# Stick-breaking values for 512 queries at a time, from turned weights in a triangular layout, with moved loads

## The chip, the core and the metric

The kernel runs on one core of one Trainium2 chip. The metric is the device time of one execution in microseconds. Of the kernel before, three runs were timed, and one more execution was profiled.

## The reference

One decoder layer, for 1024 positions of width 1024, in float32. An input projection feeds a gated linear attention (GLA, 4 heads) and a stick-breaking attention (8 heads of width 128); both are gated, projected, merged by learned gates, projected again, added to the input and normalized. Cut to what the change touches:

```python
# stick_breaking: q, k, v of 8 heads, d = 128, for blocks of 128 queries
z = einsum('bhqd,bhkd->bhqk', qb, kh[:, :, :L]) / sqrt(d)
causal = spos < tpos
log1m = where(causal, log_sigmoid(-z), 0.0)
between = cumsum(log1m, axis=3, reverse=True) - log1m
A = where(causal, exp(log_sigmoid(z) + between), 0.0)
o = einsum('bhqk,bhkd->bhqd', A, vh[:, :, :L])
...
o_sb = o_sb * silu(s_gate)                 # gate: another projection of h
merged = gates[0] * (o_gla @ w_pa) + gates[1] * (o_sb @ w_pb)
x = rmsnorm(x + merged @ w_o, final_g)
```

So a query's weight of a key is sigmoid(z) times the product of sigmoid(-z) over the keys between the two.

## The kernel before, in words

Float32 accuracy is reached with pairs: every operand is split into a rounded part (`h`) and what is left (`l`), by a copy on ACT (line 161) and a subtraction on DVE (line 162), and a product is three matmuls, h·h, h·l and l·h. The normalized input, turned, lies in four quarters `ha11`, `ha12`, `ha21`, `ha22`, each 128 x 4 x 512 for h and l.

The stages follow each other. First come the norm, the value projections and the sums S1 to S4 of the quarters. Then, to about 719 us, `Pairs`: 28 jobs of two 128-column groups by a seven-product scheme (units `u` = 0 to 6; unit 2 is the one that reads S2, line 284), with the GLA work laid between them. S1 to S4 lie in the pool `sp`; the quarter `ha21` is not read by the pairs, lies in DRAM meanwhile (`d_a21`), and comes back by two transfers of 1 MB (line 897) into a pool that is opened after `sp` is closed.

Then the stick-breaking stage, 64 steps of (head h, block i of 128 queries). A step has three parts on PE. `scores(h, i)` makes z against the keys before it, in one piece up to 512 keys and two above; ACT makes sigmoid(-z) in `eb` (line 935) and sigmoid(z) in `be` (936), DVE scans `eb` backwards into the running product (939), POOL masks the diagonal block of `be` (940), DVE multiplies (943). `turn(h, i)` turns `be` by blocks of 128 (line 958) and splits them into `ath`, `atl`. `values(h, m)` multiplies them with v for 256 queries (975 to 977), takes the gate times the result (978) and stores it. Scores run two steps ahead of the turn. Between them stand units of projection (24 matmuls of 512 columns, lines 200 to 202), taken from one long list: gates of the stick-breaking heads, then the GLA projection `w_pa`. How many stand where is written in `SB_PLAN`: for each i, so many ahead of the turn, and so many behind it. A unit's weights are loaded by `load_w` (line 177) into one of two `raw` tiles.

Last come `w_pb` with the merge, and the output projection by the seven-product scheme, with the residual x in tiles `y`, `ya` (`y_load`, line 1218), the add (1243), the sum of squares, the scale and the stores.

Within these stages a tile scheduler sets the order in which each engine gets its instructions, starting from the order of the program; in a few stretches (`manual_schedule`) ACT and DVE, in the last one PE too, keep the order written. Each engine then works through its own list in order, and each DMA is issued in the order of SP's list. A tile that takes another's place waits until the other is read.

Of the kernel before, what the change touches and what calls it, by code (L numbers as in the profile page):

```python
# [15 lines left out]
P = 128  # L16
# [19 lines left out]
SB_PLAN = [(0, 0), (0, 0), (0, 0), (0, 1), (0, 0), (0, 0), (1, 0), (0, 1)]  # L36
# [63 lines left out]
def hybrid_layer(ctx: ExitStack, tc: tile.TileContext, x, norm_g, w_in, w_up, b_dec,  # L100
# [73 lines left out]
    def load_w(w, c0, eng=nc.vector):  # L174

        raw = raw_tile()[:, :, 0:P]
# [147 lines left out]
    SLOTS = ["s2h", "s2l", "s1h", "s1l", "s3h", "s3l", "s4h", "s4l"]  # L324

    def slot(i, shape, name, dt=F32):

        n = math.prod(shape[1:])
        return (sp.tile([P, 4, HALF], dt, tag=SLOTS[i], name=name, bufs=1)
                .rearrange("p a b -> p (a b)")[0:shape[0], 0:n])  # L330
# [565 lines left out]
    for i in range(2):  # L896
        nc.sync.dma_start(hq[1, 0][i].bitcast(F32), d_a21[i])
    sb = sr_ctx.enter_context(tc.tile_pool(name="sb", bufs=2, side="right", reuse_waits="tile"))
# [46 lines left out]
    def turn(h, i):  # L945

        be = bets.pop((h, i))
        ath, atl = abuf[(i // 2 + 1) % 2]
        qc = slice((i % 2) * P, (i % 2 + 1) * P)
        s0 = 1 - i % 2  # L950
        nb = i + 1
        for b0 in range(0, nb, 4):
            bn = min(4, nb - b0)
            pt = (ps.tile([P, HALF], F32, tag="pp", name="pp", bufs=3) if b0 else
                  ps.tile([P, HALF], F32, tag="tr", name="tr"))
            for b in range(bn):
                c = T - (b0 + b + 1) * P
                nc.tensor.transpose(pt[:, b * P:(b + 1) * P], be[:, c:c + P], ident)  # L958
            ss = slice(s0 + b0, s0 + b0 + bn)
            split(pt[:, 0:bn * P].rearrange("p (a b) -> p a b", a=bn),  # L960
                  ath[:, ss, qc], atl[:, ss, qc])

    def values(h, m):

        ath, atl = abuf[(m + 1) % 2]
        v = vts[h]
        gs = slice(m * DV, (m + 1) * DV)
        gate = ev.tile([P, HALF], F32, tag="f", name="f")[:, 0:DV]
        nc.sync.dma_start(gate, d_sg[h][:, gs])
        pav = ps.tile([P, HALF], F32, tag="av", name="av", bufs=1)  # L970
        ns = 2 * m + 2
        for s in range(ns):
            j = 2 * m + 1 - s
            vh, vl = (v[j // 4][:, j % 4, e] for e in range(2))
            nc.tensor.matmul(pav[:, 0:DV], vh, ath[:, s], start=s == 0, stop=False)  # L975
            nc.tensor.matmul(pav[:, 0:DV], vh, atl[:, s], start=False, stop=False)  # L976
            nc.tensor.matmul(pav[:, 0:DV], vl, ath[:, s], start=False, stop=s == ns - 1)  # L977
        nc.vector.tensor_mul(gate, pav[:, 0:DV], gate)
        nc.sync.dma_start(d_osb[h][:, gs], gate)
# [18 lines left out]

    def load(w, c0, key):
# [377 lines left out]
```

## Time and profile before

| | |
|---|---|
| median of 3 runs | 1217.54 us (1216.15 to 1218.54) |
| profiled execution, its own time | 1220.86 us |
| its span, first to last instruction | 1219.1 us |
| PE (matmul) busy | 1202.0 us, 99% |
| DVE busy | 793.8 us, 65% |
| ACT busy | 540.7 us, 44% |
| mean DMA rate | 198 GB/s |
| granted TensorE clock, mean | 0.996 |

PE is TensorE's matmuls, PEld its weight loads, DVE VectorE, ACT ScalarE, POOL GpSimd, SP the engine that issues nearly all DMAs. In a group's row stand line, engine, operation, the names out<-in, shapes and count; then busy us and mean ns of one; then the idle time ahead of them and what ended it. In a row of a stretch stand its bounds, its length, the busy time of PE, PEld, DVE, ACT and POOL (with counts), the granted clock, the DMA engines' share and GB/s. A row in order of time has start, length, engine, line and operation; in brackets the idle time before it.

### The profile page before, as it was taken

The numbers are of one execution on the slowest core, as the hardware profiler recorded it, in microseconds if no ns is written. First come the engines' busy times: TensorE is split into PE (matmuls) and PEld (weight loads), VectorE is DVE, ScalarE is ACT, GpSimd is POOL, SyncE is SP. The second block draws the span as 40 slices with busy tenths as digits, with TensorE's granted clock in tenths as the row PEclk, the third lists the DMA queues.
The fourth block names the chain that finished last, engine by engine and source line by source line (L and its number), as shares of the span: only waits on it lengthen the run. The fifth ranks groups of instructions, "written<-read, shape, count | busy, mean of one in ns | idle before, by whom it ended". The sixth has DMA issues, their size and how long they took to land.

```text
span 1219.1 us, 17810 instructions
## 1 busy us (share of the span) xinstructions
PE 1202.0 (99%) x6327; PEld 1019.6 (84%) x6327; DVE 793.8 (65%) x1285; ACT 540.7 (44%) x1045; POOL 323.3 (27%) x303
## 2 busy tenths in 40 slices
PE   8999999999999999999999999999999999999997
PEld 8999878888888888888888878888888888888876
DVE  5575875675766566766765437777687875345676
ACT  5344663334334444454443325454455554332343
POOL 1495523322422324223223211111121110033201
PEclk9999999999999999999999999999999999999999
DMA  7544348866656547657554395545896636667653
GB/s 278 186 143 140 147 169 293 278 205 190 203 155 203 175 143 231 201 191 228 171 180 146 118 321 165 191 141 163 277 300 218 198 131 226 199 213 248 243 192 121
DMA packets 209236, 241.41 MB, mean 198 GB/s; under 512 B 12758, under 2 KB 152044, under 8 KB 207100
## 3 DMA queue, kind: packets, MB, share of 16 engines
q1 hardware_dynamic: 208572, 239.23, 60.0%
q8 instruction: 50, 0.82, 0.3%
q10 hardware_dynamic: 576, 1.05, 0.2%
q14 instruction: 38, 0.31, 0.1%
HBM read 149.53 MB, written 90.70 MB: 197 GB/s over the span
## 4 chain that ended last, share of the span: by engine, by line
PE 83%; issue 7%; DVE 4%; ACT 2%; DMA 2%; POOL 1%; SPq 0%; POOLq 0%; ACTq 0%; DVEq 0%
PE pp L266 13%; PE pp L268 13%; PE pp L267 13%; PE pp L219 8%; PE pp L202 6%; PE pp L201 5%; PE pp L200 5%; PE tr L958 1%; PE xb L1235 1%; PE xb L1236 1%; PE xb L1234 1%; PE av L976 1%; POOL be L940 1%; PE pp L1234 1%; DVE eb L939 1%
## 5 line engine op out<-in xcount | busy, mean ns | idle before, releaser
L940 POOL TENSOR_SCALAR_AFFINE_SELECT be<-be 128x128 f32<-128x128 f32 x64 | 44.9, 701 | 235.4 <-ACT be L936 204.3
L305 DVE TENSOR_TENSOR f<-pp,f 128x512 f32<-128x512 f32 x84 | 57.9, 689 | 73.3 <-PE pp L268 67.8
L162 DVE TENSOR_TENSOR wl<-tt,wh 128x1024 fp32r<-128x1024 f32 x56 | 69.6, 1243 | 53.1 <-ACT wh L161 52.8
L162 DVE TENSOR_TENSOR wl<-raw,wh 128x1024 fp32r<-128x1024 f32 x55 | 75.9, 1381 | 42.6 <-ACT wh L161 41.8
L161 ACT ACTIVATE wh<-raw 128x1024 fp32r<-128x1024 f32 x55 | 58.1, 1058 | 93.7 <-PE pp L267 47.0
L939 DVE TENSOR_TENSOR_SCAN eb<-eb,m 128x128 f32<-128x128 f32 (+3 forms) x64 | 86.8, 1358 | 15.8 <-ACT eb L935 15.7
L240 POOL TENSOR_TENSOR tt<-raw 128x512 f32<-128x512 f32 x28 | 39.1, 1397 | 205.1 <-DVE wl L162 198.5
L161 ACT ACTIVATE wh<-tt 128x1024 fp32r<-128x1024 f32 x56 | 59.3, 1059 | 67.9 <-PE pp L267 67.3
L272 ACT ACTIVATE f<-pp 128x512 f32<-128x512 f32 x84 | 49.7, 592 | 79.5 <-PE pp L268 76.2
L227 POOL TENSOR_TENSOR r<-r,nhalf 128x1 f32<-128x1 f32 x40 | 24.3, 607 | 191.9 <-DVE r L226 178.5
L935 ACT ACTIVATE eb<-z 128x384 f32<-128x384 f32 (+4 forms) x96 | 48.0, 500 | 47.0 <-issue 22.0
L585 ACT ACTIVATE o<-o,vcol 128x512 f32<-128x512 f32 x32 | 23.0, 724 | 62.0 <-DMA o<-d_gb 40.4
L943 DVE TENSOR_TENSOR be<-be,eb 128x128 f32<-128x128 f32 (+3 forms) x64 | 48.3, 756 | 3.1 <-DVE eb L939 0.5
L200 PE MATMUL pp<-bh,wh 128*128 128x512 f32 x128 | 49.8, 389 | 0.0
L201 PE MATMUL pp<-bl,wh 128*128 128x512 f32 x128 | 49.8, 389 | 0.0
L202 PE MATMUL pp<-bh,wl 128*128 128x512 f32 x128 | 49.8, 389 | 0.0
L936 ACT ACTIVATE be<-z 128x384 f32<-128x384 f32 (+4 forms) x96 | 48.3, 503 | 0.0
L976 PE MATMUL av<-atl,v 128*128 128x256 f32 x160 | 46.0, 288 | 2.0 <-DVE atl L162 2.0
L975 PE MATMUL av<-ath,v 128*128 128x256 f32 x160 | 47.3, 295 | 0.0
L1125 POOL TENSOR_TENSOR f<-m 128x512 f32<-128x512 f32 x8 | 14.2, 1771 | 118.8 <-DVE m L1115 118.8
L977 PE MATMUL av<-ath,v 128*128 128x256 f32 x160 | 45.3, 283 | 0.0
L266 PE MATMUL pp<-ha22h,wh 128*128 128x512 f32 x112 | 44.5, 397 | 0.2 <-DVE f L305 0.2
(430 smaller groups left out, 4014.9 us busy)
## 6 DMA issues: line engine op xcount, KB each, us to landing
raw<-in_w_in_dram SPq DMA_DIRECT2D x31, 1024.0 KB, 6.2
d_v<-o SPq DMA_DIRECT2D x32, 256.0 KB, 2.9
d_gv<-o SPq DMA_DIRECT2D x32, 256.0 KB, 3.6
v<-d_gv SPq DMA_DIRECT2D x32, 256.0 KB, 3.0
d_ogl<-o SPq DMA_DIRECT2D x64, 128.0 KB, 2.5
d_q<-o SPq DMA_DIRECT2D x16, 512.0 KB, 4.8
d_k<-o SPq DMA_DIRECT2D x16, 512.0 KB, 4.1
k<-d_k SPq DMA_DIRECT2D x8, 1024.0 KB, 5.6
```

Source lines behind the costliest of these rows:

```text
L161: nc.scalar.activation(hi, src, AF.Copy)
L162: eng.tensor_sub(lo, src, hi.bitcast(F32))
L200: nc.tensor.matmul(pt, whi[:, kb], h_, start=kb == 0, stop=False)
L201: nc.tensor.matmul(pt, whi[:, kb], l_, start=False, stop=False)
L202: nc.tensor.matmul(pt, wlo[:, kb], h_, start=False, stop=kb == KB - 1)
L219: nc.tensor.matmul(pt[:, 0:n], *ops[kb][i], start=k == 0, stop=k == 3 * KB - 1)
L266: nc.tensor.matmul(pt, bh[:, j], ah[:, j], start=first and j == 0, stop=False, skip_group_check=True)
L267: nc.tensor.matmul(pt, bh[:, j], al[:, j], start=False, stop=False, skip_group_check=True)
L268: nc.tensor.matmul(pt, bl[:, j], ah[:, j], start=False, stop=j == 3, skip_group_check=True)
L305: nc.vector.tensor_add(add, bank, add)
L939: nc.vector.tensor_tensor_scan(rest, rest, m1[:, off:T][:, ::-1], 1.0, op0=ALU.mult, op1=ALU.max)
L976: nc.tensor.matmul(pav[:, 0:DV], vh, atl[:, s], start=False, stop=False)
```

## The change

**Values by 512 queries.** `values(h, g)` takes a group g of four blocks. For the second group, the four key blocks of the first group are products of 512 columns (`far`). In the group's own four blocks, key block k has queries only from block k on: 512, 384 and 256 columns, and 256 again for the last, of which the first 128 are zeros. The weights lie in `near` as 13 blocks of 128, row k behind row k-1 in steps of three, so that block (k, q) stands at 3k + q and each row is one contiguous run; block 11 is set to zero once. `turn` writes the own group's blocks from a `tr` bank and the far ones from a `pp` bank. There are two `near` pairs, one for each group; that of the first lies in the tiles `tt` and `raw` that the pairs have left. The two weight loads in flight take the two halves of the other `raw` tile. Queries are loaded for two blocks at once, into the tiles `dh` and `dl` of the pairs. `SB_PLAN` is another: three units a head as before, now one each behind the turns of blocks 2, 4 and 7.

**The fourth quarter.** S2 lies in a pool `a21b` that stays open, and `ha21` takes its place: its load is given out four units before the end of the pairs, ahead of the first head's k and v.

**The last residual rows.** The rows of (1, 3) get the tiles `dh` and `dl`, and are loaded with the others; residual rows are loaded, scaled and stored by halves of 512 columns.

In the lists of the engines this is what stands at three places. First PE, at the end of a head of the stick-breaking stage; `z` are scores, `tr` and `pp` from `ident,be` turns, `pp` from `ha..,wh` a unit. Before, from the last score matmul of block 7 on:

```order
L933 MATMUL z<-k,q 128x512
L958 MATMUL tr<-ident,be 128x128 x4
L958 MATMUL pp<-ident,be 128x128 x2
L931 MATMUL z<-k,q 128x256
L932 MATMUL z<-k,q 128x256
L933 MATMUL z<-k,q 128x256
L200 MATMUL pp<-ha11h,wh 128x512
L201 MATMUL pp<-ha11l,wh 128x512
L202 MATMUL pp<-ha11h,wl 128x512
```

The rest of that unit follows, 24 matmuls in all, then the turn of block 6, 18 value matmuls, one score of the next head, and the turn of block 7. Now, from the same matmul on:

```order
L946 MATMUL z<-k,q 128x512
L968 MATMUL tr<-ident,be 128x128 x2
L968 MATMUL pp<-ident,be 128x128 x4
L944 MATMUL z<-k,q 128x256
L945 MATMUL z<-k,q 128x256
L946 MATMUL z<-k,q 128x256
L968 MATMUL tr<-ident,be 128x128 x3
L968 MATMUL pp<-ident,be 128x128 x4
L944 MATMUL z<-k,q 128x256
L945 MATMUL z<-k,q 128x256
L946 MATMUL z<-k,q 128x256
L968 MATMUL tr<-ident,be 128x128 x4
```

The turn of block 7 (last row) has moved to directly behind the turns of 5 and 6 and two scores; the unit stands behind it. In some heads a third score stands before the last row.

DVE at the same place, from the gate product of the values on. Before, and then now:

```order
L978 TENSOR_TENSOR f<-av,f 128x256
L939 SCALAR_TENSOR_TENSOR eb_7321<-eb_7321,m_7322 128x1024
L162 TENSOR_TENSOR atl_7333<-tr,ath_7332 128x4x128
L943 TENSOR_TENSOR be<-be,eb_7321 128x1024
L162 TENSOR_TENSOR atl_7333<-pp,ath_7332 128x2x128
```

```order
L162 TENSOR_TENSOR wl<-raw,wh 128x1024
L566 TENSOR_TENSOR o<-pp,o 128x512
L992 TENSOR_TENSOR f<-av,f 128x512
L952 SCALAR_TENSOR_TENSOR eb_7319<-eb_7319,m_7320 128x1024
L162 TENSOR_TENSOR atl<-tr,ath 128x2x128
L956 TENSOR_TENSOR be<-be,eb_7319 128x1024
```

Between scan and product of block 7 one low part of the turned weights stands in both; it has 256 columns now, 512 before.

SP, at the load of the fourth quarter, before and then now:

```order
L897 DMA ha21h<-d_a_166 128x2048
L578 DMA d_ga_149<-f 128x512
L578 DMA d_ga_148<-f 128x512
L897 DMA ha21l<-d_a_167 128x2048
L177 DMA raw<-in_w_in_dram 128x8x128
L565 DMA d_sg_100<-o 128x512
L886 DMA q<-d_q_76 128x2x128 x3
```

```order
L899 DMA ha21h<-d_a_166 128x2048
L899 DMA ha21l<-d_a_167 128x2048
L580 DMA d_ga_149<-f 128x512 x2
L891 DMA q<-d_q_76 128x2x256
L580 DMA d_ga_148<-f 128x512
L891 DMA q<-d_q_76 128x2x256
```

Both parts of the quarter now stand ahead of the last stores of the pairs, the first queries behind them.

The diff, cut to its core:

```diff
-SB_PLAN = [(0, 0), (0, 0), (0, 0), (0, 1), (0, 0), (0, 0), (1, 0), (0, 1)]
+SB_PLAN = [(0, 0), (0, 0), (0, 1), (0, 0), (0, 1), (0, 0), (0, 0), (0, 1)]
...
+    a21b = ctx.enter_context(tc.tile_pool(name="a21b", bufs=1, side="right", reuse_waits="tile"))
     s_ctx = ExitStack()
...
-                comb[nm] = quarter(sp, nm, nm.lower())
+                comb[nm] = quarter(a21b, nm, "a21") if nm == "S2" else quarter(sp, nm, nm.lower())
...
-    def load_q(h, i):
-        qts[h, i] = sl.tile([P, 2, P], F32R, tag="q", name="q", bufs=3)
-        nc.sync.dma_start(qts[h, i].bitcast(F32), d_q[h][:, :, i * P:(i + 1) * P])
+    def load_q(h, m):
+
+        tag = "d" + "hl"[m % 2]
+        t = sw.tile([P, 4, P], F32R, tag=tag, name="q", bufs=1).rearrange("p a c -> p (a c)")
+        t = t.rearrange("p (s c) -> p s c", s=2)
+        nc.sync.dma_start(t.bitcast(F32), d_q[h][:, :, m * DV:(m + 1) * DV])
+        for e in range(2):
+            qts[h, 2 * m + e] = t[:, :, e * P:(e + 1) * P]
...
-    load_head(0)
-    for s in range(3):
-        load_q(*steps[s])
-    pairs.run()
-    s_ctx.close()
-    a21b = ctx.enter_context(tc.tile_pool(name="a21b", bufs=1, side="right", reuse_waits="tile"))
+    pairs.run(7 * len(pairs.jobs) - 4 - pairs.at)
     hq[1, 0] = quarter(a21b, "ha21", "a21")
     for i in range(2):
         nc.sync.dma_start(hq[1, 0][i].bitcast(F32), d_a21[i])
+    load_head(0)
+    pairs.run()
+    for m in range(2):
+        load_q(0, m)
+    s_ctx.close()
...
-    abuf = [tuple(sb.tile([P, KB - 2 * i, 2 * P], F32R, tag=f"at{s}{i}", name=f"at{s}{i}", bufs=1)
-                  for s in "hl") for i in range(2)]
-    for pair in abuf:
+    wraw = raw_tile()
+    near = [(sw.tile([P, 4 * HALF], F32R, tag="tt", name="ath", bufs=1),
+             sw.tile([P, 4 * HALF], F32R, tag="raw", name="atl", bufs=2)),
+            tuple(sb.tile([P, 13 * P], F32R, tag="at" + s, name="at" + s, bufs=1) for s in "hl")]
+    near = [[a[:, 0:13 * P].rearrange("p (b c) -> p b c", c=P) for a in pair] for pair in near]
+    far = [sb.tile([P, 4, HALF], F32R, tag="af" + s, name="af" + s, bufs=1) for s in "hl"]
+    for pair in near:
         for a in pair:
-            nc.gpsimd.memset(a[:, 0, 0:P].bitcast(F32), 0.0)
+            nc.gpsimd.memset(a[:, 11].bitcast(F32), 0.0)
...
     def turn(h, i):
 
         be = bets.pop((h, i))
-        ath, atl = abuf[(i // 2 + 1) % 2]
...
+        g, q = divmod(i, 4)
+        L = (i + 1) * P
+
+        def go(tag, keys, dst):
+            pt = ps.tile([P, HALF], F32, tag=tag, name=tag, bufs=BANKS.get(tag, 2))
+            for b, k in enumerate(keys):
+                c = T - L + k * P
                 nc.tensor.transpose(pt[:, b * P:(b + 1) * P], be[:, c:c + P], ident)
...
+            split(pt[:, 0:len(keys) * P].rearrange("p (a b) -> p a b", a=len(keys)), *dst)
+
+        go("tr", range(4 * g, i + 1), [a[:, q:4 * q + 1:3] for a in near[g]])
+        if g:
+            go("pp", range(4), [a[:, :, q * P:(q + 1) * P] for a in far])
+
+    def values(h, g):
+
         v = vts[h]
...
+        ops = [(k, pav, far[0][:, k], far[1][:, k]) for k in range(4)] if g else []
+        for k in range(4):
+            q = min(k, 2)
+            ops.append((4 * g + k, pav[:, q * P:HALF],
+                        *(a[:, 3 * k + q:3 * k + 4].rearrange("p b c -> p (b c)") for a in near[g])))
+        for s, (k, out_, ah, al) in enumerate(ops):
...
+            nc.tensor.matmul(out_, vh, ah, start=first, stop=False, skip_group_check=True)
+            nc.tensor.matmul(out_, vh, al, start=False, stop=False, skip_group_check=True)
+            nc.tensor.matmul(out_, vl, ah, start=False, stop=last, skip_group_check=True)
+        nc.vector.tensor_mul(gate, pav, gate)
+        nc.sync.dma_start(d_osb[h][:, half(g)], gate)
...
-        if s + 3 < len(steps):
-            load_q(*steps[s + 3])
+        if i % 2 and s + 3 < len(steps):
+            h2, i2 = steps[s + 3]
+            load_q(h2, i2 // 2)
...
-        if i % 2 == 0 and s:
-            values(*((h, i // 2 - 1) if i else (h - 1, 3)))
-    values(SB_H - 1, 3)
+        if i % 4 == 0 and s:
+            values(*((h, 0) if i else (h - 1, 1)))
+    values(SB_H - 1, 1)
...
     def y_load(n, t):
-        ys[n, t] = (po.tile([P, D], F32, tag="ya", name="ya", bufs=4) if n == 0 or t == 3 else
-                    py.tile([P, D], F32, tag="y", name="y"))
...
+        if (n, t) == (1, 3):
+            ys[n, t] = [sw.tile([P, 4, P], F32, tag="d" + s, name="yd", bufs=1).rearrange("p a c -> p (a c)")
+                        for s in "hl"]
...
-    for t in range(3):
+    for t in range(4):
         y_load(1, t)
...
-        if k == 15:
-            y_load(1, 3)
```

Lines behind the change move: 200 to 202 stay, the scores' 931 to 933 are 944 to 946, the scan 952, the product 956, the transposes 968, the values 989 to 991.

More of the change, by code (lines that the diff above doesn't have):

```diff
@@ L947, in turn @@
         be = bets.pop((h, i))
-        ath, atl = abuf[(i // 2 + 1) % 2]
[L949 to L961, printed above, removed]
@@ L966, in values @@
+        if g:
+            go("pp", range(4), [a[:, :, q * P:(q + 1) * P] for a in far])
+    def values(h, g):
         v = vts[h]
-        gs = slice(m * DV, (m + 1) * DV)
-        gate = ev.tile([P, HALF], F32, tag="f", name="f")[:, 0:DV]
-        nc.sync.dma_start(gate, d_sg[h][:, gs])
+        gate = ev.tile([P, HALF], F32, tag="f", name="f")
+        nc.sync.dma_start(gate, d_sg[h][:, half(g)])
         pav = ps.tile([P, HALF], F32, tag="av", name="av", bufs=1)
[L971 to L977, printed above, removed]
@@ L978, in values @@
-        nc.vector.tensor_mul(gate, pav[:, 0:DV], gate)
-        nc.sync.dma_start(d_osb[h][:, gs], gate)
+        ops = [(k, pav, far[0][:, k], far[1][:, k]) for k in range(4)] if g else []
[4 more added lines that the diff above has]
+        for s, (k, out_, ah, al) in enumerate(ops):
+            vh, vl = (v[k // 4][:, k % 4, e] for e in range(2))
+            first, last = s == 0, s == len(ops) - 1
+            nc.tensor.matmul(out_, vh, ah, start=first, stop=False, skip_group_check=True)
+            nc.tensor.matmul(out_, vh, al, start=False, stop=False, skip_group_check=True)
+            nc.tensor.matmul(out_, vl, ah, start=False, stop=last, skip_group_check=True)
@@ L997, in hybrid_layer, with go @@
     ws = {}
+    wk = []
     def load(w, c0, key):
-        return (lambda: ws.__setitem__(key, load_w(w, c0)), False)
+        def go():
+            raw = wk.pop(0) if wk else None
+            ws[key] = load_w(w, c0, raw=raw)
+            if raw is not None:
+                wk.append(raw)
+        return (go, False)
     def unit(key, quads, n, fn):
@@ L1046, in hybrid_layer @@
     st = Line(line)
+    wk += [wraw.rearrange("p k c -> p (k c)")[:, i * KB * P:(i + 1) * KB * P].rearrange("p (k c) -> p k c", c=P)
+           for i in range(2)]
     st.run(2)
@@ L1214, in y_load @@
     def y_load(n, t):
[L1215 to L1216 removed]
+        if (n, t) == (1, 3):
+            ys[n, t] = [sw.tile([P, 4, P], F32, tag="d" + s, name="yd", bufs=1).rearrange("p a c -> p (a c)")
+                        for s in "hl"]
+        else:
+            y = (po if n == 0 else py).tile([P, D], F32, tag="y", name="y", bufs=4 - n)
+            ys[n, t] = [y[:, half(J)] for J in range(2)]
         r0 = n * HALF + t * P
[L1218 removed]
+        for J in range(2):
+            nc.sync.dma_start(ys[n, t][J], x2[r0:r0 + P, half(J)])
     for t in range(4):
```

42 lines of the change are left out of this document (20 added, 22 removed).

## The prediction

> **What bounds the kernel now.** I read the span and the shares of busy time first.
>
> ```profile
> span 1219.1 us, 17810 instructions
> PE 1202.0 (99%) x6327; PEld 1019.6 (84%) x6327; DVE 793.8 (65%) x1285; ACT 540.7 (44%) x1045; POOL 323.3 (27%) x303
> ```
>
> PE is busy for 1202.0 of 1219.1 us, so two things alone move the end: PE time that is saved, and PE time that stands still. DVE, with 65%, has slack on average; whether it has any at one place must be read there. So next came the waits of PE from 690 to 1060 us, the whole stick-breaking stage with what leads into it (waited for, total, times, longest), and then stretches of 5 and 10 us around each wait, with PE's busy time in the second column and the granted clock in the third from the end.
>
> ```profile
> PE av L976 <- DVE atl L162: 2.0, 7, 0.3
> PE pp L201 <- DMA ha21l<-d_a: 2.0, 1, 2.0
> ```
>
> ```profile
> 725.00:730.00 5.00, 3.00 (x16) 2.14 (x16) 3.75 (x7) 2.47 (x7) 1.60 (x3) 1.00 0.91 310
> 730.00:735.00 5.00, 5.00 (x16) 3.95 (x15) 0.00 (x0) 0.00 (x0) 0.00 (x0) 0.66 0.69 217
> 770.00:775.00 5.00, 4.73 (x29) 3.81 (x29) 3.29 (x5) 3.07 (x8) 1.52 (x2) 1.00 0.78 266
> 1180.00:1190.00 10.00, 9.26 (x41) 7.34 (x40) 6.75 (x10) 2.62 (x4) 0.55 (x1) 1.00 0.36 141
> 10.00:20.00 10.00, 7.36 (x39) 6.34 (x38) 7.16 (x11) 5.30 (x10) 1.10 (x2) 0.83 1.05 405
> ```
>
> Little is left to win from waits: 2.0 us for the fourth input quarter, seven of about 0.3 us at the second value matmul, and one of 0.74 us near the end (1180 to 1190). But a wait can cost more than its length. After the 2.0 us wait the stretch from 730 to 735 ran at a mean clock of 0.66; if the low clock is half, that is 0.34/0.5 x 5 = 3.4 us at half rate, or 1.7 us of PE work lost. The matmuls show it: they follow at about 0.23 us before, and at 0.43 us in it.
>
> ```profile
> 729.18 0.50 PE L201 MATMUL pp<-ha21l,wh 128*128 128x512 f32 x1 [1.99 <-DMA ha21l<-d_a]
> ...
> 730.57 0.63 PE L200 MATMUL pp<-ha21h,wh 128*128 128x512 f32 x1
> 731.00 0.63 PE L201 MATMUL pp<-ha21l,wh 128*128 128x512 f32 x1
> ```
>
> The stretch 10 to 20 us, with 2.64 us of PE idle, shows the same sign (0.83: 1.7 us lost). Waits of 0.3 and 0.74 us leave the clock at 1.00. So somewhere between 0.74 and 2.0 us of standing still, about 1.7 us more has to be paid.
>
> **The change part by part. Values by 512 queries.** What a matmul costs is the distance to the next start, since they overlap. The first row below is one of the three groups of value matmuls, the others are starts.
>
> ```profile
> L976 PE MATMUL av<-atl,v 128*128 128x256 f32 x160 | 46.0, 288 | 2.0 <-DVE atl L162 2.0
> ```
>
> ```profile
> 790.22 0.39 PE L200 MATMUL pp<-ha12h,wh 128*128 128x512 f32 x1
> ...
> 792.03 0.39 PE L202 MATMUL pp<-ha12h,wl 128*128 128x512 f32 x1
> 793.14 0.28 PE L976 MATMUL av<-atl,v 128*128 128x256 f32 x1
> ...
> 795.06 0.28 PE L977 MATMUL av<-ath,v 128*128 128x256 f32 x1
> ```
>
> Eight starts of 512 columns take 1.81 us, 0.226 each; sixteen of 256 take 1.92, 0.120 each; 384 columns, halfway between, I take at 0.173. Before: 480 value matmuls of 256 (three lines, 160 each) are 57.6 us. Now each head has 18 of 512, 6 of 384 and 12 of 256: 4.07 + 1.04 + 1.44 = 6.55 us, and eight heads 52.4. PE saves **5.2 us**. The number of transposes, of score matmuls and of projection matmuls is the same. The halved number of gate loads, value stores and gate products takes work from SP, DMA and DVE, which do not bound on average: nothing by itself.
>
> **The seven waits at the second value matmul** go: the diagonal values now start a whole step and 24 projection matmuls after the transposes of their last block, and no longer right behind them. **2.0 us** saved.
>
> **The fourth input quarter** is loaded into the place of the sum S2 as soon as the third product of the last pair has read it, and its second part no longer waits for the sums' pool to be given up.
>
> ```profile
> 708.29 0.39 PE L268 MATMUL pp<-S2h,wl 128*128 128x512 f32 x1
> ...
> 721.31 0.42 SPq L897 DMA_DIRECT2D ha21l<-d_a  x1
> ...
> 724.84 0.39 PE L200 MATMUL pp<-ha21h,wh 128*128 128x512 f32 x1
> ```
>
> ```profile
> ha21l<-d_a SPq DMA_DIRECT2D x1, 1024.0 KB, 7.8
> ```
>
> The last reading of S2 starts at 708.29; a transfer of 7.8 us issued then lands around 716 and the second one, sharing the engines, some microseconds later, before PE wants the quarter at 724.84. Now the second part is issued at 721.31. The wait of 2.0 and the half clock of 1.7 go: **3.7 us**. What hides the load are the last four units of that pair; if SP comes to the issue late, up to the same 3.7 stays.
>
> **The last residual rows** get two tiles of their own and are loaded with the others. At present their transfer starts when an output store has landed, the add that needs it comes late, and PE waits:
>
> ```profile
> 1182.88 0.33 SPq L1218 DMA_DIRECT2D ya<-in_x_dram  x1
> ...
> 1187.19 0.50 PE L1234 MATMUL pp<-wB22h,mS4h 128*128 128x512 f32 x1 [0.74 <-DVE ya L1243]
> ```
>
> **0.7 us** saved. Handling rows by halves adds eight loads, four stores and four products on DVE, with the same bytes and columns, at a place where PE waits for nothing else. I take nothing for it; the final products stand off PE's path behind the last matmul as before.
>
> Saved in all: 5.2 + 2.0 + 3.7 + 0.7 = **11.6 us**.
>
> **The new table of units.** This is what costs. Of a head's eight steps, 0 to 7, the units of projection stand behind the turns of steps 2, 4 and 7 now; the one ahead of step 6's turn is gone. So between the scores of step 7 (1024 keys) and the transposes of its weights, PE has two turns and two small scores, no projection. Before, a whole unit and 18 value matmuls stood there too. The present trace gives the length of both sides:
>
> ```profile
> 855.40 0.39 PE L933 MATMUL z<-k,q 128*128 128x512 f32 x1
> 855.63 0.60 PE L958 MATMUL tr<-ident,be 128*128 128x128 f32 x4
> 856.15 0.61 ACT L935 ACTIVATE eb<-z 128x512 f32<-128x512 f32 x1
> 856.32 0.39 PE L931 MATMUL z<-k,q 128*128 128x256 f32 x1
> 856.54 0.28 PE L932 MATMUL z<-k,q 128*128 128x256 f32 x1
> ...
> 857.40 2.28 DVE L939 TENSOR_TENSOR_SCAN eb<-eb,m 128x1024 f32<-128x1024 f32 x1
> ...
> 860.17 1.22 DVE L943 TENSOR_TENSOR be<-be,eb 128x1024 f32<-128x1024 f32 x1
> 861.31 0.42 DVE L162 TENSOR_TENSOR atl<-pp,ath 128x256 fp32r<-128x256 f32 x1
> 862.27 0.60 PE L958 MATMUL tr<-ident,be 128*128 128x128 f32 x4
> ...
> 862.95 0.36 PE L975 MATMUL av<-ath,v 128*128 128x256 f32 x1
> ...
> 865.55 0.60 PE L958 MATMUL tr<-ident,be 128*128 128x128 f32 x4
> ```
>
> The chain, from the start of the last score matmul (855.40): the second sigmoid ends at 856.76, 1.36 later; the scan takes 2.28, a low part of 256 columns, which now stands between scan and product on DVE, 0.42, the product 1.22: 5.28, less some 0.1 for each of two DVE instructions that start before the one ahead has ended (861.31 begins before 860.17 + 1.22): 5.1 us. In the present order the product ended at 861.39 and the transposes came at 865.55; 4.2 us of slack. PE's cover in the new order: the last score and six transposes, 855.40 to 856.32, 0.92; a 256-wide score, 0.46 (0.22 for its first matmul, 0.12 for two more); seven transposes, 0.68 (862.27 to 862.95); one more 256-wide score, 0.46. Together 2.52 us. **PE stands still for 5.1 - 2.5 = 2.6 us in each head.** In the last head no scores of a next one follow, the cover is 0.92 + 0.68 = 1.6, and it waits 3.5. Seven times 2.6 and 3.5: **21.7 us** lost. Behind the waiting transposes stand, in PE's one queue, the 24 matmuls of the unit, so nothing fills the hole. From below, with the low part of 256 hidden and no delay between engines, the chain is 0.39 + 0.61 + 2.28 + 1.22 = 4.5 and the wait 2.0, 17 us in all; from above, a DVE that has just begun a split of weights (the row below) when the scan is due would make it 3.8, 31 us. I stay at 21.7, since in the printed order that split stands three places ahead of the scan.
>
> ```profile
> L162 DVE TENSOR_TENSOR wl<-tt,wh 128x1024 fp32r<-128x1024 f32 x56 | 69.6, 1243 | 53.1 <-ACT wh L161 52.8
> ```
>
> **The clock.** Each new wait is longer than the 2.0 us that was followed by 3.4 us at half rate. A wait that falls into two of the clock's stretches may escape, so I count six of eight at 1.6 us: **9.6 us**, as an estimate; none and all (13.6) are the ends. Here the Trainium skill says otherwise: by its page "TensorE: Matmul & The Clock Gate", "Why this matters for your kernels", only gaps of more than about 3 us between matmuls drop the rate. Here a wait of 1.99 us was followed by the half rate, so the trace does not agree; by the page's rule seven of the eight waits would cost only their length.
>
> Sum against the profiled execution: -11.6 + 21.7 + 9.6 = +19.7 us. Its span of 1219.1 becomes 1238.8. That execution took 1220.9 us, 3.3 above the median of the runs shown (1217.5), so the median becomes 1237.2, **1237 us**.
>
> **The rivals.** *The waits come, the clock holds.* For it: a wait that is cut by the edge of a clock stretch, and the seven short waits without effect. Against it: both places with about 2 us of idle PE lost clock. It gives -11.6 + 21.7 = +10.1: 1227.6 us. The rule of the Trainium skill's page "TensorE: Matmul & The Clock Gate" leads to this outcome too.
>
> *The cover suffices after all: faster.* The place is the turn of step 7; the mechanism would be a chain that ends within PE's cover. It decides where the wait and its lost clock fall below 11.6/8 = 1.45 us a head, a chain under 4.0 us without any lost clock. For it: DVE is at 65%, and the slack is 4.2 us now. Against it: the four durations alone sum to 4.5, and the scan, one instruction over 1024 columns, can't begin before the last sigmoid. Price: all 11.6 us, 1205.9.
>
> *The quarter is still late.* The DMA engines are full where it is loaded (0.91 of their time from 725 to 730), and the first queries of the stage are now issued behind the quarter and wait for the last pair's fourth part. If quarter or queries come late, the 3.7 us are not saved: 1240.9; with the same again for the queries about 1245. Against it: the load has some 16 us, 708 to 724.8, for 8.
>
> **How the numbers follow.** About 0.2% (2.4 us) is what a measurement of this kernel can tell from no change. The forecast (waits with lost clock, 1231 to 1243) 0.60; clock holds 0.20; quarter late or more DVE delay (1241 to 1248) 0.12; cover suffices 0.05; a sum near zero by shorter waits 0.03. So slower 0.92, same 0.03, faster 0.05. The range 1225 to 1245 leaves out the faster rival and the far end of the upper one. Its low end is the short wait of 17 us with no lost clock: -11.6 + 17 = +5.4, 1222.9, taken up by 2 since both at once is unlikely; the high end is all eight clock losses, 13.6, with 26 us of waits: +28.
>
> **What would show it.** In the new profile PE's longest wait must be transposes (line 968) for DVE's product of `be` (line 956), eight times, 2 to 3.5 us, with the granted clock under 1.00 in the stretches behind. The value matmuls must sum to about 52 us, the waits of PE for the fourth quarter and for the last rows must be gone. I am wrong if those transposes start without a wait of at least 1.5 us, or if the clock stays at 1.00 behind them.

## The result and the profile after

The changed kernel takes 1238.6 us (median of six runs, 1236.2 to 1240.1) against 1217.8 us before: a ratio of 1.017, with a 95% interval of 1.015 to 1.018. It is slower by 1.7%. The prediction was 1237.

The profiled execution of the changed kernel has a span of 1236.0 us (before: 1219.1) at a mean granted clock of 0.992 (before: 0.996). The first rows of its page:

```profile
span 1236.0 us, 17257 instructions
PE 1202.4 (97%) x6135; PEld 1012.3 (82%) x6135; DVE 792.9 (64%) x1273; ACT 541.0 (44%) x1045; POOL 310.3 (25%) x303
```

PE has 192 instructions fewer and is busy just as long. That is no contradiction: at half clock the matmuls follow each other at about twice the distance, and all of it counts as busy. The waits of PE from 690 to 1080 us (waited for, total, times, longest):

```profile
PE tr L968 <- DVE be L956: 18.5, 9, 3.5
PE z L944 <- DMA q<-d_q: 1.7, 2, 0.9
```

The seven waits at the second value matmul, the one for the fourth quarter and the one near the end (1080 to 1236 us shows none) are gone. In their place stand the transposes of step 7, line 968, that wait for DVE's product of `be`. This is the first head's turn of step 7 as the timeline has it:

```profile
751.44 0.39 PE L945 MATMUL z<-k,q 128*128 128x512 f32 x1
751.67 0.39 PE L946 MATMUL z<-k,q 128*128 128x512 f32 x1
...
752.90 0.61 ACT L949 ACTIVATE be<-z 128x512 f32<-128x512 f32 x1
...
753.06 2.29 DVE L952 TENSOR_TENSOR_SCAN eb<-eb,m 128x1024 f32<-128x1024 f32 x1 [0.99 <-ACT eb L948]
...
754.05 0.28 PE L946 MATMUL z<-k,q 128*128 128x256 f32 x1
...
755.27 0.40 DVE L162 TENSOR_TENSOR atl<-tr,ath 128x256 fp32r<-128x256 f32 x1
755.58 1.21 DVE L956 TENSOR_TENSOR be<-be,eb 128x1024 f32<-128x1024 f32 x1
...
756.94 0.63 PE L968 MATMUL tr<-ident,be 128*128 128x128 f32 x4 [2.61 <-DVE be L956]
```

From the last score matmul (751.67) to the end of the product (756.79) are 5.12 us: two sigmoids, a scan of 2.29, a low part of 0.40, a product of 1.21. PE had work up to 754.33. The rest is the wait of 2.61.

What each of those waits did to the clock is read from stretches around them (length, busy time of PE, PEld, DVE, ACT and POOL, then granted clock, DMA share, GB/s):

```profile
755.00:760.00 5.00, 3.06 (x18) 2.71 (x19) 5.00 (x10) 2.25 (x6) 0.73 (x2) 1.00 0.87 300
830.00:835.00 5.00, 4.70 (x18) 4.13 (x19) 4.45 (x10) 1.85 (x4) 0.29 (x1) 0.66 0.85 304
868.00:873.00 5.00, 4.13 (x22) 3.57 (x23) 5.00 (x10) 1.75 (x4) 0.29 (x1) 1.00 1.03 385
905.00:910.00 5.00, 4.13 (x16) 3.69 (x17) 5.00 (x10) 1.85 (x4) 0.29 (x1) 0.66 1.05 406
980.00:985.00 5.00, 4.34 (x16) 3.85 (x17) 4.81 (x10) 2.46 (x5) 0.29 (x1) 0.66 0.19 66
1018.00:1025.00 7.00, 6.04 (x19) 5.11 (x20) 3.87 (x6) 1.80 (x3) 0.00 (x0) 0.51 0.65 221
```

A wait of the same 2.61 us stands in front of the first five. Two of them (755, 868) leave the clock at 1.00, three are followed by 0.66, which is 3.4 us at half rate. Behind the last, 3.46 us long, the half rate lasts 6.8 us. Together 17.1 us at half rate, 8.5 us of PE work lost.

**Where the 16.9 us of span come from.** PE is the bound, so the distance from each matmul's start to the next one's, added up by kind over all that start after 700 us, accounts for the whole (us; worked out from the starts in the two traces; a wait counts to the matmul ahead of it):

```
kind                       before   after   difference
value matmuls                60.3    53.4      -6.9
projections of the units    271.4   270.6      -0.8
scores                       56.4    74.7     +18.3
transposes                   27.2    35.2      +8.0
seven-product products       96.3    94.5      -1.8
sum                         511.6   528.4     +16.8
```

The last kind is the output projection with the end of the pairs; its -1.8 holds the wait of 0.7 us for the last rows and about 0.7 us of three products that here stand just before 700 us. The hole stands behind the scores and between the transposes. The half clock falls on the transposes and projections behind it, which is why the projections gain almost nothing although the wait for the quarter is gone.

### The profile page after: what moved, and what is told of

It is laid out like the page before. It is cut to its first block, busy times and chain, and to the rows that moved or that the text cites. A ratio compares the mean times of both kernels' runs of the same rounds, so it can differ in the third digit from the quotient of the medians.

```text
span 1236.0 us, 17257 instructions
## 1 busy us (share of the span) xinstructions
PE 1202.4 (97%) x6135; PEld 1012.3 (82%) x6135; DVE 792.9 (64%) x1273; ACT 541.0 (44%) x1045; POOL 310.3 (25%) x303
## 4 chain that ended last, share of the span: by engine, by line
PE 88%; DVE 5%; ACT 3%; issue 2%; DMA 2%; SPq 0%; POOL 0%; ACTq 0%; DVEq 0%; POOLq 0%
PE pp L266 13%; PE pp L268 13%; PE pp L267 13%; PE pp L219 8%; PE pp L200 7%; PE pp L202 7%; PE pp L201 7%; DVE eb L952 1%; PE av L989 1%; PE av L991 1%; PE av L990 1%; PE tr L968 1%; PE z L944 1%; PE xb L1269 1%; PE xb L1267 1%
## 5 line engine op out<-in xcount | busy, mean ns | idle before, releaser
L953 POOL TENSOR_SCALAR_AFFINE_SELECT be<-be 128x128 f32<-128x128 f32 x64 | 32.5, 508 | 265.7 <-ACT be L949 226.8
L968 PE MATMUL tr<-ident,be 128*128 128x128 f32 x160 | 29.3, 288 | 18.5 <-DVE be L956 18.5
L266 PE MATMUL pp<-ha11h,wh 128*128 128x512 f32 x112 | 44.6, 399 | 0.0
L266 PE MATMUL pp<-S1h,wh 128*128 128x512 f32 x112 | 44.5, 397 | 0.0
```

Of the source, the lines that this page charges most:

```text
L266: nc.tensor.matmul(pt, bh[:, j], ah[:, j], start=first and j == 0, stop=False, skip_group_check=True)
```

## The experiments

**1. The unit ahead of step 7's turn.** One entry of the table:

```diff
-SB_PLAN = [(0, 0), (0, 0), (0, 1), (0, 0), (0, 1), (0, 0), (0, 0), (0, 1)]
+SB_PLAN = [(0, 0), (0, 0), (0, 1), (0, 0), (0, 1), (0, 0), (0, 0), (1, 0)]
```

> The changed kernel with one entry of its table altered: step 7's unit of projection stands ahead of the turn instead of behind it. Theory (the turn of step 7 waits because nothing covers the chain of 5.1 us): the unit's 24 matmuls, 24 x 0.226 = 5.4 us, fill the wait of 2.6 to 3.5 us in every head; about 20 us of waits and 8.5 us at half clock go, and the saved 11.6 us show: 1238.6 - 20.2 - 8.5 = 1210, down to 1206 by the sum of the prediction, so faster than before by 0.6 to 1.0%. Rival (the cost sits in another part of the change, such as the query loads or the layout): it stays above 1230.

Measured: 1210.5 us, ratio to the kernel before 0.994 (0.993 to 0.996). The same kernel timed again, as the base of experiments 4 to 6:

> The changed kernel with step 7's unit ahead of its turn, the same as before, timed again as the base of the next two. Expected: 1210.5, faster than the kernel before by 0.4 to 0.7%.

Measured: 1209.4 us, ratio 0.993 (0.992 to 0.995). The waits of PE from 715 us on, and a stretch over the first head's turn of step 7, in the first of the two profiles:

```profile
PE z L944 <- ACT be L949: 0.6, 1, 0.6
PE av L989 <- ACT afh L161: 0.6, 1, 0.6
PE tr L968 <- DVE be L956: 0.2, 1, 0.2
```

```profile
756.86 1.22 DVE L956 TENSOR_TENSOR be<-be,eb 128x1024 f32<-128x1024 f32 x1
...
760.69 0.40 PE L202 MATMUL pp<-ha12h,wl 128*128 128x512 f32 x1
760.93 0.60 PE L968 MATMUL tr<-ident,be 128*128 128x128 f32 x4
```

The product ends at 758.08, and the transposes come at 760.93, behind the 24 matmuls of the unit: 2.9 us of slack in place of a wait of 2.6. The wait, the lost clock and 28 us of time go with one entry of the table; the 20.2 us of waits and 8.5 us of clock read above make 28.7. The rival, a cost in another part of the change, asked for 1230 or more and falls. The rest of the change is a gain, and this version is faster than both kernels.

**2. The other two tables, in both kernels.** In the changed kernel the table of before:

```diff
-SB_PLAN = [(0, 0), (0, 0), (0, 1), (0, 0), (0, 1), (0, 0), (0, 0), (0, 1)]
+SB_PLAN = [(0, 0), (0, 0), (0, 0), (0, 1), (0, 0), (0, 0), (1, 0), (0, 1)]
```

> The changed kernel with the table of the kernel before (units behind the turns of steps 3 and 7 and ahead of that of step 6). Theory: the table is what makes the wait, so with the old one the cover ahead of step 7's turn is 2.5 + 5.4 = 7.9 us for a chain of 5.1 and no wait over 1 us is left there: 1206 to 1213, where other turns may wait up to 0.7 us. Rival (the layout of the weights or the moved values make the wait whatever the table): the time stays at 1230 or more.

Measured: 1215.0 us, ratio 0.998 (0.997 to 0.999). The rival falls, and no wait over 1 us is left, but the time is 2 us above the upper end expected. Of the waits of PE from 715 us on, the largest sum and the longest single one:

```profile
PE tr L968 <- DVE atl L162: 1.9, 6, 0.5
PE pp L200 <- DVE o L566: 0.9, 1, 0.9
```

In the kernel before, the table of the change (the same diff turned round):

> The kernel before with only the table of the change. Theory of the prediction refined: ahead of step 7's turn there still stand 18 value matmuls of 256 columns (18 x 0.120 = 2.2 us) beside the 2.5 us of scores and transposes, so the wait is only 5.1 - 4.7 = 0.4 us, up to 1.6 if DVE is late, and the clock holds: 1221 to 1231. The full cost needs both, the table and the moved values. Rival (the table alone has the whole cost): 1217.8 + 21.7 + 9.6 = 1249.

Measured: 1231.7 us, ratio 1.012 (1.010 to 1.014). And in the kernel before, the table of experiment 1:

> The kernel before with only the table altered, to units behind the turns of steps 2 and 4 and ahead of that of step 7. Theory: the good table is no gain by itself; step 7's turn has 2.5 + 2.2 + 5.4 = 10 us of cover already, and the second value matmul of a step still waits for its weights, seven times 0.3 us or more (1.3 with the table of the change). 1218 to 1228. Rival (the gain of the changed kernel with this table comes from the table, not from the values by 512 queries and the early loads): it reaches 1212.

Measured: 1228.2 us, ratio 1.008 (1.007 to 1.010). All six (us):

```
table of units               kernel before   changed kernel
of before (3, 6 ahead, 7)        1217.8          1215.0
of the change (2, 4, 7)          1231.7          1238.6
experiment 1 (2, 4, 7 ahead)     1228.2      1210.5 and 1209.4
```

No table is good or bad by itself. The one that serves the changed kernel best costs the kernel before about 10 us. With the table of the change the kernel before does not wait at step 7's transposes but, as the waits show, at its second value matmul:

```profile
PE av L976 <- DVE atl L162: 9.1, 8, 1.5
```

```profile
755.42 2.29 DVE L939 TENSOR_TENSOR_SCAN eb<-eb,m 128x1024 f32<-128x1024 f32 x1 [0.76 <-ACT eb L935]
755.85 0.49 PE L958 MATMUL pp<-ident,be 128*128 128x128 f32 x3
756.43 0.39 PE L975 MATMUL av<-ath,v 128*128 128x256 f32 x1
757.63 0.67 DVE L162 TENSOR_TENSOR atl<-tr,ath 128x512 fp32r<-128x512 f32 x1
...
758.35 0.39 PE L976 MATMUL av<-atl,v 128*128 128x256 f32 x1 [1.30 <-DVE atl L162]
```

The low part of the weights is queued on DVE behind the same kind of scan, one of 2.29 us. So the same cause, a long scan with too little PE work beside it, comes out as another wait. My upper end of 1231 for this run was just missed, as was that of 1228 for the other table; I had asked only what the transposes wait for, not what DVE's queue holds up behind the scan. Six of these eight waits are 1.30 to 1.54 us long, two 0.5, and no half clock follows any of them. With the table of experiment 1 the second value matmul waits seven times 0.62 us, and one wait of 1.84 us, for ACT, has 3.4 us at half clock behind it.

From 690 us on, the listed waits and clock losses explain about 6 of the 11.0 us that the span grows by with the one table, and 3 of the 8.5 with the other. A listed wait counts from the end of a matmul that overlaps its successor by 0.16 us, so shorter stalls do not show in the list at all. The starts show them: after 700 us the matmuls fall behind their usual steps (0.226 us for 512 columns, 0.120 for 256) by 10.9 and 8.2 us more than in the kernel before, and in 88 and 96 places by over 0.1 us each, where it has 54. So the remaining 5 us too are PE standing still, in many short stalls; what PE waits for in each of them was not followed up.

**3. Idle matmuls in the hole.** In the six heads whose turn waits 2.6 us or more, ten (then five) matmuls whose result is never read:

```diff
         st.run(SB_PLAN[i][0])
+        if i == 7 and h not in (1, 5):
+            idle = ps.tile([P, HALF], F32, tag="av", name="av", bufs=1)
+            for _ in range(10):
+                nc.tensor.matmul(idle, kts[h][:, 0, 0:P], kts[h][:, 0, 0:HALF], start=True, stop=True)
         turn(h, i)
```

> The changed kernel with ten idle matmuls of 512 columns (10 x 0.226 = 2.26 us, their result is never read) ahead of step 7's turn in the six heads that wait 2.6 us or more; they take up time that PE stands still anyway and add no work to the end of the chain. Theory (a wait costs its length and about 8.5 us more by half clock behind it): the wait of the turn keeps its end, but PE idles only 0.4 us, the clock stays at 1.00 and the time falls by up to 8.5 us, to 1230. By the rule of the Trainium skill's page 'TensorE: Matmul & The Clock Gate', 'Why this matters for your kernels' (only gaps over about 3 us count), one of the waits alone, the last of 3.46 us, costs clock. Rival (the half clock is not caused by the idle time): 1238 to 1239, with the same stretches at half clock.

Measured: 1233.0 us (1230.5 to 1234.3), ratio 1.013 (1.011 to 1.014). That is 5.6 us less than the changed kernel, with 60 matmuls more. The clock is 1.00 in every stretch behind a filled hole; it falls only at 795 us, in one of the two heads left alone, behind two waits of 0.82 and 0.94 us close together, and in the first 20 us:

```profile
788.00:800.00 12.00, 10.24 (x54) 8.65 (x53) 9.68 (x15) 6.67 (x16) 1.78 (x4) 0.86 0.56 199
1011.00:1020.00 9.00, 7.82 (x46) 6.49 (x45) 7.11 (x9) 5.40 (x11) 0.29 (x1) 1.00 0.90 307
```

The loss here is two stretches, 3.4 us, where the changed kernel lost 8.5: 5.1 us, against 5.6 measured. The 1230 expected, with nothing lost, was missed by these two stretches. With five in place of ten:

> The changed kernel with five idle matmuls (5 x 0.226 = 1.1 us, result never read) ahead of step 7's turn in six heads: PE's idle time there falls from 2.6 to about 1.5 us, the turn itself starts no earlier. Theory (a stretch of 3.4 us is followed by half clock when PE idles in more than about half of it, 1.7 us, as in the runs so far): the clock holds in those six heads though most of the wait is still there, and the time is that of ten idle matmuls, 1231 to 1234. Rival (the clock falls behind any wait over about 1 us): 1238 as without them.

Measured: 1231.9 us (1231.8 to 1233.5), ratio 1.012 (1.010 to 1.014), 6.7 us less than the changed kernel. Now PE still waits in every head, and the clock holds all the same, but for the last head, where 2.31 us were left:

```profile
PE tr L968 <- DVE be L956: 10.8, 9, 2.3
```

```profile
826.00:834.00 8.00, 6.56 (x40) 5.53 (x40) 7.62 (x12) 4.57 (x12) 1.26 (x3) 1.00 0.91 311
1011.00:1020.00 9.00, 6.69 (x28) 5.17 (x27) 5.96 (x8) 3.14 (x7) 0.00 (x0) 0.81 0.74 248
```

One stretch at half clock in place of five: 4 x 1.7 = 6.8 us, against the 6.7 measured (by the ratios to the kernel before it is 5.9, so the agreement is good to about 1 us). So the cost of the clock is shown apart from that of the wait: from the last score matmul to the turn the first head takes 5.27 us in the changed kernel (751.67 to 756.94) and 5.28 with ten idle matmuls (752.67 to 757.95), so the chain is the same and only PE's idle time differs. The rival, half clock for another reason, falls, and so does the one of the second run, that any wait over about 1 us costs clock.

**4. The fourth quarter.** With the table of experiment 1, first the load written behind the last pair and the queries:

```diff
-    hq[1, 0] = quarter(a21b, "ha21", "a21")
-    for i in range(2):
-        nc.sync.dma_start(hq[1, 0][i].bitcast(F32), d_a21[i])
     load_head(0)
     pairs.run()
     for m in range(2):
         load_q(0, m)
     s_ctx.close()
+    hq[1, 0] = quarter(a21b, "ha21", "a21")
+    for i in range(2):
+        nc.sync.dma_start(hq[1, 0][i].bitcast(F32), d_a21[i])
```

> The version with step 7's unit ahead of its turn, and in it the fourth quarter's load issued where the kernel before had it, behind the whole last pair and the first queries. Theory (the early load saves the wait of 2.0 us and the 1.7 us at half clock behind it): PE waits for the quarter again, 2 to 3 us, and the time rises by 3.7 us, to 1214. Rival (the quarter's place costs nothing or the saved time lies elsewhere): within 1 us of the base.

Measured: 1211.2 us (1210.7 to 1211.9), ratio 0.995 (0.993 to 0.996). The edit did not do what it was to do. The lists of PE and SP came out the same as the base's, instruction for instruction, and the place that the quarter takes was as free as before:

```profile
707.27 0.39 PE L268 MATMUL pp<-S2h,wl 128*128 128x512 f32 x1
...
707.69 0.39 SPq L904 DMA_DIRECT2D ha21h<-d_a  x1
708.13 0.43 SPq L904 DMA_DIRECT2D ha21l<-d_a  x1
```

Both parts are issued within 0.9 us of the start of the last reading of S2, as in the base (708.60 and 709.07 behind 708.12 there). So this run is a repeat of the base, and it shows what repeats differ by: 1210.5, 1209.4 and 1211.2 us, with one event in its profile that the base's two do not show. An activation stood 4.48 us in ACT's queue waiting for a gate's transfer, the sigmoids of a score behind it, and PE waited 1.6 us for them:

```profile
923.95 0.72 ACT L587 ACTIVATE o<-o,vcol 128x512 f32<-128x512 f32 x1 [4.48 <-DMA o<-d_ga]
924.57 0.58 ACT L948 ACTIVATE eb<-z 128x512 f32<-128x512 f32 x1
```

Differences under about 2 us between versions are therefore not told apart by their times. The true undoing gives S2 its own places back and lets the quarter's pool open when the sums' pool closes:

```diff
-    a21b = ctx.enter_context(tc.tile_pool(name="a21b", bufs=1, side="right", reuse_waits="tile"))
     s_ctx = ExitStack()
...
-    SLOTS = ["a21h", "a21l", "s1h", "s1l", "s3h", "s3l", "s4h", "s4l"]
+    SLOTS = ["s2h", "s2l", "s1h", "s1l", "s3h", "s3l", "s4h", "s4l"]
...
-                comb[nm] = quarter(a21b, nm, "a21") if nm == "S2" else quarter(sp, nm, nm.lower())
+                comb[nm] = quarter(sp, nm, nm.lower())
...
     s_ctx.close()
+    a21b = ctx.enter_context(tc.tile_pool(name="a21b", bufs=1, side="right", reuse_waits="tile"))
+    hq[1, 0] = quarter(a21b, "ha21", "a21")
```

> The version with step 7's unit ahead of its turn, and in it S2 with places of its own in the sums' pool and the fourth quarter in a pool that opens only when that pool closes, as in the kernel before. Theory: the second part of the quarter is again issued some 13 us after the last reading of S2, PE waits about 2 us for it and runs 3.4 us at half clock behind it: plus 3.7 us, about 1213.5. Rival (a wait there is covered, or only its length counts): 1209 to 1211.5.

Measured: 1212.2 us (1210.4 to 1214.6), ratio 0.995 (0.994 to 0.997), 1.8 us above the mean of the three base medians (1210.4), and with a spread of 4.2 us where the base has 1.1 to 1.9. That is between the 1213.5 of the theory and the 1211.5 of the rival, and the times alone do not decide. The wait is back:

```profile
717.78 0.65 SPq L903 DMA_DIRECT2D ha21h<-d_a  x1
720.45 0.74 SPq L903 DMA_DIRECT2D ha21l<-d_a  x1
...
725.97 0.47 PE L200 MATMUL pp<-ha21h,wh 128*128 128x512 f32 x1 [1.82 <-DMA ha21h<-d_a]
```

In this profile, which is of the fastest of its runs, no half clock follows (the stretch 730 to 735 has 1.00; of the wait, 1.54 us lie within one of the clock's steps, which the last section explains). So the early load saves the wait, and the 1.7 us of clock not in every execution: the profile of the kernel before has them, this one does not.

**5. The last residual rows.** With the table of experiment 1, the rows (1, 3) again in a tile that an earlier output row gives up, loaded late:

```diff
-        if (n, t) == (1, 3):
-            ys[n, t] = [sw.tile([P, 4, P], F32, tag="d" + s, name="yd", bufs=1).rearrange("p a c -> p (a c)")
-                        for s in "hl"]
+            y = po.tile([P, D], F32, tag="y", name="y", bufs=4)
+            ys[n, t] = [y[:, half(J)] for J in range(2)]
...
+        if k == 15:
+            y_load(1, 3)
```

> The version with step 7's unit ahead of its turn, and in it the last residual rows again loaded into a tile that an earlier output row gives up. Theory: the wait of 0.7 us of the final products comes back, the clock holds, and the time rises by 0.7 us (0.06%, less than these rounds can tell; the trace decides). Rival (the handling by halves, more loads and stores, costs time itself): the wait comes back but nothing is lost, or the base has waits of its own at the end.

Measured: 1211.2 us (1210.0 to 1216.7), ratio 0.995 (0.993 to 0.997). A wait comes back, of 0.2 us and not the 0.7 expected (rows are now stored and loaded by halves; whether that is why was not tried):

```profile
PE pp L1267 <- DVE y L1275: 0.2, 1, 0.2
```

That edit is worth a few tenths of a microsecond, less than repeats differ by.

**6. The first microseconds.** With the table of experiment 1, ten idle products in the place of four where PE waits for its first inputs:

```diff
-WARM = (13, 4)
+WARM = (13, 10)
```

> The version with step 7's unit ahead of its turn, and ten idle transposing products in the place of four in the first microseconds, where PE waits 1.3 and 0.7 us for the first split inputs and a stretch at half clock follows in most runs. Theory: six more, 6 x 0.107 = 0.6 us, cut the first wait to 0.7, less than half a stretch idles, and the 1.7 us at half clock are saved: 1208 to 1209. Rival (the idle products delay the first real ones, or the clock is lost all the same): 1210 to 1211.

Measured: 1211.0 us (1210.3 to 1211.7), ratio 0.994 (0.993 to 0.996). The time is no better than the base: the rival holds. The profile has no half clock at the start, but five of the other twelve profiles have none there either, without this edit, so that it was the edit is not shown. Each product stands in the trace as two instructions of 0.107 us, so the six more took 1.3 us and not the 0.6 expected. The wait of 1.3 us for `ha11l` at 11.3 us is gone, and others stand in its place, 1.3 us for the first transposes (0.6 in the base) and 0.9 for a later part of `ha11l` at 26.9 us.

## Why the prediction was right, point by point

- **Values by 512 queries**: 5.2 us and 2.0 us of waits forecast, 6.9 in all measured (60.3 to 53.4). The steps per matmul hold: the twelve matmuls of a group's own blocks, three of 512, three of 384 and six of 256 columns, are 3 x 0.226 + 3 x 0.173 + 6 x 0.120 = 1.92 us by the prediction's steps, and take 1.93 (748.58 to 750.51).

```profile
748.58 0.39 PE L989 MATMUL av<-ath,v 128*128 128x512 f32 x1
...
750.39 0.28 PE L991 MATMUL av<-ath,v 128*128 128x256 f32 x1
750.51 0.40 PE L944 MATMUL z<-k,q 128*128 128x512 f32 x1
```

- **The new wait**: the chain was forecast at 5.1 and is 5.12; the wait at 2.6 and 3.5, and is 2.61 and 3.46. In two of eight heads, though, it is 0.86 + 0.90. There a 384-column score of the next head stood ahead of the turn, which the count of cover had not in it, and that score itself had to wait for its query's load:

```profile
789.03 0.52 SPq L891 DMA_DIRECT2D q<-d_q  x1
...
792.13 0.41 PE L944 MATMUL z<-k,q 128*128 128x384 f32 x1 [0.86 <-DMA q<-d_q]
...
793.79 0.66 PE L968 MATMUL tr<-ident,be 128*128 128x128 f32 x4 [0.90 <-DVE be L956]
```

  The sum is 20.2 us in place of 21.7. Experiment 1 shows that the cause is the missing cover and that the unit ahead of the turn removes it; the old table in the changed kernel removes it too.

- **The clock**: 9.6 forecast, 8.5 measured. The guess that some waits escape was right; I counted six of eight, and it was four: two of the six long waits were cut by the edge of a clock stretch, the two heads with a split wait lost nothing, and the last wait cost two stretches. So that 8.5 came so near to 9.6 is partly luck. The Trainium skill's page "TensorE: Matmul & The Clock Gate", "Why this matters for your kernels", warns only of gaps of more than about 3 us. The traces do not agree that shorter ones are free: three waits of 2.61 us were each followed by 3.4 us at half rate, and experiment 3 takes the loss away with the idle time.

- **The fourth quarter**: 3.7 forecast, 2.0 for the wait and 1.7 for the clock. The wait is gone. The 1.7 is where the profiled execution before misled: it lost 3.4 us to half clock, at the start and at the quarter, and took 1220.9 us, 3.1 above the median. Other executions need not lose either: of 33 of the kernel before whose clock is on record, nine have a mean clock of 0.999, too high for even one such stretch beside the half clock behind the last matmul (2.1 to 5.0 us in the thirteen traces), and spans of 1214.4 to 1216.6 us.

- **From the span to the median**: I took it that the profiled execution of the changed kernel would lie as far above its median as that of the kernel before. It lies 0.9 us below, and so the medians differ by 20.8 us and the two profiled executions by 16.9. The sum of 19.7 was 2.8 us too high for the profiled executions, and the step to the median 4.0 us too low. The two nearly cancelled. That 1237 is only 1.4 us from the measured 1238.6 is therefore luck in part; the mechanism is not.

- **The last rows**: 0.7 forecast, the wait is gone; that the halves cost nothing was not tried by itself, since experiment 5 keeps them.

- **Rivals.** "The clock holds" would have been 1227.6 and falls. "The cover suffices" was not so for this table, but its price, 1205.9, is near what experiment 1 gives (1209.4 to 1210.5): without the wait the rest of the change saves 7 to 8 us in the medians and 9.2 to 10.7 in the spans, not 11.6. Added up from the starts as above, the values save 6.5 us, the projections with the fourth quarter 5.1 to 5.7 and the products at the end 0.7 to 0.8, but scores and transposes take 2.0 to 2.7 us longer; and the lost clock that the sum took off is not lost in every execution. "The quarter is still late" falls: its first matmul starts without a wait.

The mechanism was right. The terms that were mis-sized are the cover in two heads (20.2 us of waits for 21.7) and the number of waits that cost clock (8.5 for 9.6); together 2.6 us too much, with 1.7 us of half clock at the start that this execution of the changed kernel happened not to lose. Smaller losses, 0.16 us or so per wait beyond its listed length, ran the other way.

## What to carry to other kernels

When work is moved in an engine's queue, take the longest chain of another engine that ends at this place, sum the work that is left beside it in the new order, and the difference is the wait; here that gave 2.6 us against 2.61 measured, in five of the seven heads for which it was worked out. Do it for every consumer of that other engine's queue, not only for the one that the change names: with another layout the same scan held up another instruction. And try the table and the layout together, since a table that costs one layout 10 us served the other one best.

## What the runs showed of the hardware that was not expected

The granted clock changes on a grid of 3.413 us that runs free of the program: in the nine of the thirteen traces that have more than one stretch of half clock, each begins at a whole number of such steps from the first one of its execution. The Trainium skill's page "TensorE: Matmul & The Clock Gate", "What's actually happening", states such a free-running window of 3413 ns, and the traces agree. For a fall it asks for a whole idle window, and there they do not. What goes with a fall here is PE's idle time inside one step, not the length of a wait. From the starts and ends of the matmuls in all thirteen traces, for steps that end before the last matmul does:

```
idle time of PE within one step of 3.413 us      clock in the next step
21 steps with 1.25 to 1.59 us idle                full in all
 4 steps with 1.70, 1.72, 1.73 and 1.76 us        half, half, full, half
12 steps with 1.78 to 2.67 us                     half in all
```

Of the over 4500 steps with less idle time, up to 1.11 us, the next is at full clock in all but one. The edge is near half a step, 1.7 us. Experiment 3 cut five waits from 2.61 to about 1.44 us in their place, and no half clock followed any of the five. A wait of 2.61 us that the grid cuts into 1.02 and 1.59 costs nothing (at 756.9), the same wait inside one step costs 1.7 us more (at 830.3), and two waits of 0.82 and 0.94 us within one step cost as much as a long one. Where the grid's edges fall differs from execution to execution (the first half clock of the start begins at 12.7 to 13.9 us in seven traces), so the same kernel can lose more or less: the six executions of the changed kernel have spans from 1234.4 us at a mean clock of 0.993 to 1238.4 us at 0.989, where 0.004 of 1236 us is 4.9 us. That the clock makes all of this spread is not shown, since a mean clock also counts the half clock behind the last matmul, 2.8 us in the profiled execution, which delays no matmul. One thing stays open: behind the last head's wait of 3.46 us two steps ran at half clock, though the second of them followed one with only 0.8 us idle.
